# Two small first units of h in the input projection, and S5's constants made in steps beside later units

## The chip, the cores and the metric

The kernel runs on one core of a Trainium2 chip. The metric is the device time of one execution in microseconds. Its engines are named PE (TensorE, matrix products, with PEld for its weight loads), DVE (VectorE), ACT (ScalarE), POOL (GpSimd) and SP (SyncE, which here only issues transfers).

## The reference

One decoder layer on x of 256 tokens by 4096 features, all in float32:

```
shift, scale, gate = split(silu(c) @ W_ada + b_ada)       # W_ada 4096 x 12288
h = x * (1 + scale) + shift
q, k, v, g_lr, z_gla, u_s5, z_s5 = split(h @ W_in)        # W_in 4096 x 10256
o_gla = RMSNorm_head(GLA(q, k, v, alpha(g_lr))) * silu(z_gla)
o_s5  = GLU(gelu(Re(C s) + D u_s5)) * silu(z_s5)          # s: complex diagonal scan
x = LayerNorm(alpha_dn * x + gate * (concat(o_gla, o_s5) @ W_out))
```

The scan of S5 runs over groups with 64 complex states each. Its constants come from lambda and log_dt of each group: exp(lambda * dt), its powers up to the fourth, and the factor (exp(lambda * dt) - 1) / lambda.

## The kernel before

**Input projection.** h has 4096 features, 32 tiles of 128 rows (k tiles). They are made in eight *units* of four k tiles. W_in's columns are cut into 21 *chunks* of 512 columns (list KINDS; the chunk with the first head's v is cut in two, of 256 and 272 columns). A *visit* of a chunk (`win_chunk`) multiplies the k tiles of one unit, or of two units, with the chunk's weights, sums in PSUM, and at its end copies (first visit, ScalarE, L220) or adds (later visits, VectorE, L222) the sum into an accumulator in SBUF. The weights of two k tiles and one chunk are a *piece* of 512 KB: one transfer (L83, queue SP, six buffers), one cast to its high part on ScalarE (L114), one subtraction for its low part on VectorE (L115), and 12 products (L211), since float32 is made of high x high, low x high and high x low.

The plan (`win_plan`) walks through the units. In unit b some chunks are visited for unit b - 1 and unit b together, others for unit b alone. PAIRED says how many chunks share a visit at each border of two units: 6, 7, 7, 7, 7, 8, 7. So 119 visits in all.

**h.** For each unit `ada_steps` fetches x on GpSimd's queue (L161) and 32 pieces of W_ada, 512 KB each (`ada_sums`, 128 rows by 512 shift and 512 scale columns). VectorE multiplies each piece with a column of silu(c) and adds it to `rows` (L151 for the first, L153 for the others). TensorE sums `rows` over its partitions with a column of ones (L166), VectorE adds the bias (L169, L170), ScalarE makes the four tiles of h (L175) and their high parts (L176), VectorE the low parts (L177). Unit 0 is made ahead of all visits. The steps of the next unit (33: one for each piece and one for the rest) are put between the visits of the unit before, evenly by interpolation over `marks`, with a lead of ADA_LEAD = 1, which is two weight pieces ahead here. `rows` has one buffer.

**S5's constants.** `s5_params` fetches lambda and log_dt (tile lam), computes on VectorE in scratch tiles of 64 to 128 columns (tile s5scratch, lines 255 to 380), and clears pad and w0 on GpSimd (L385). It is emitted whole behind unit 0's h. `later(LATE)` lowers its priority by 60 places, and a scheduler puts its instructions between those of the projection.

**Order.** Each engine's order of instructions is fixed when the kernel is built: a list scheduler takes them by priority, which is the order of emission but for `later`, beside a simulated timeline.

Behind the projection's S5 chunks and beside its last unit come the inputs and the scan of S5, the GLA heads, the pieces of W_ada for gate, and then the products with W_out and the GLU.

Of the kernel before, what the change touches and what calls it, by code (L numbers as in the profile page):

```python
# [11 lines left out]
F32R = mybir.dt.float32r  # L12
# [6 lines left out]
P = 128  # L19
# [16 lines left out]

ADA_LEAD = 1
# [4 lines left out]
PAIRED = (6, 7, 7, 7, 7, 8, 7)  # L42
# [15 lines left out]
class Emit:  # L58
# [84 lines left out]
    def ada_sums(self, piece):  # L143

        nc = self.nc
        self.rows = rows = self.tmp([P, 1024], "rows")
        for kt in range(32):
            t = self.raw([P, 1024], self.io["ada"][piece, kt])
            c = self.silu_c[:, kt : kt + 1]
            if kt == 0:  # L150
                nc.vector.tensor_scalar(out=rows, in0=t, scalar1=c, scalar2=None, op0=ALU.mult)  # L151
            else:
                nc.vector.scalar_tensor_tensor(out=rows, in0=t, scalar=c, in1=rows, op0=ALU.mult, op1=ALU.add)  # L153
            yield

    def ada_steps(self, unit):

        nc, io = self.nc, self.io
        xs = [self.tmp([P, 2, SEQ], "x") for _ in range(2)]
        for i in range(2):  # L160
            nc.gpsimd.dma_start(out=xs[i], in_=io["xT"][:, unit * 4 + 2 * i : unit * 4 + 2 * i + 2, :])  # L161
        yield from self.ada_sums(unit)
        ps = self.xbank([P, 2, 4, 64])[:, :, :, 0]
        for s in range(2):
            for kt in range(4):
                nc.tensor.matmul(ps[:, s, kt : kt + 1], lhsT=self.rows[:, 512 * s + kt * P : 512 * s + kt * P + P],  # L166
                                 rhs=self.ones[:, 0:1], start=True, stop=True)
        m1 = self.tmp([P, 2, 4], "m1")
        nc.vector.tensor_tensor(out=m1, in0=ps, in1=self.bada[:, :, unit * 4 : unit * 4 + 4], op=ALU.add)  # L169
        nc.vector.tensor_scalar(out=m1[:, 1], in0=m1[:, 1], scalar1=1.0, scalar2=None, op0=ALU.add)  # L170
        hi = self.slot([P, 4, SEQ], F32R, "hhi")
        lo = self.slot([P, 4, SEQ], F32R, "hlo")
        for kt in range(4):
            x = xs[kt // 2][:, kt % 2]
            nc.scalar.activation(out=x, in_=x, func=AF.Identity, scale=m1[:, 1, kt : kt + 1], bias=m1[:, 0, kt : kt + 1])  # L175
            nc.scalar.copy(out=hi[:, kt], in_=x)  # L176
            nc.vector.tensor_tensor(out=lo[:, kt], in0=x, in1=hi[:, kt].bitcast(F32), op=ALU.subtract)  # L177
        self.h[unit] = (hi, lo)
        yield
# [12 lines left out]
    def win_chunk(self, idx, units, first, last):  # L192

        nc, io = self.nc, self.io
        kind, i = KINDS[idx]
        w = WIDTHS.get(kind, 512)
        ps = self.banks()
        for n, unit in enumerate(units):
            hhi, hlo = self.h[unit]
            for half in range(2):  # L200
                src = io[f"w_{kind}"][2 * unit + half] if kind in WIDTHS else io["w_in"][idx - 2 * (idx > FIRST_V), 2 * unit + half]
                whi, wlo = self.split(self.raw([P, 2, w], src))

                todo = [(m, kt, t, r) for ts in (((hhi, whi), (hlo, whi)), ((hhi, wlo),)) for m in range(2) for kt in range(2) for t, r in ts]
                begun, left = set(), [t[0] for t in todo]
                for m, kt, t, r in todo:
                    left.remove(m)
                    st = n + half == 0 and m not in begun
                    en = n == len(units) - 1 and half == 1 and m not in left
                    begun.add(m)  # L210
                    nc.tensor.matmul(ps[:, m, 0:w], lhsT=t[:, 2 * half + kt, m * P : m * P + P], rhs=r[:, kt], start=st, stop=en)  # L211
        if kind == "va":
            parts = [(self.acc["v"][0][:, :, 0:256], ps[:, :, 0:256])]
        elif kind == "vb":
            parts = [(self.acc["v"][0][:, :, 256:512], ps[:, :, 0:256]), (self.glr, ps[:, :, 256:272])]
        else:
            parts = [(self.acc[kind][i], ps)]
        for d, p in parts:
            if first:
                nc.scalar.copy(out=d, in_=p)  # L220
            else:
                nc.vector.tensor_tensor(out=d, in0=p, in1=d, op=ALU.add)  # L222
# [27 lines left out]
    def exp_exact(self, out, x, t):  # L250
# [8 lines left out]
        v.scalar_tensor_tensor(out=r, in0=n, scalar=2.12194440e-4, in1=r, op0=ALU.mult, op1=ALU.add)  # L259
        v.tensor_scalar(out=p, in0=r, scalar1=1.0 / 5040, scalar2=None, op0=ALU.mult)  # L260
        for k in (720, 120, 24, 6, 2, 1):
            v.scalar_tensor_tensor(out=p, in0=p, scalar=1.0 / k, in1=r, op0=ALU.add, op1=ALU.mult)
        v.tensor_scalar(out=p, in0=p, scalar1=1.0, scalar2=None, op0=ALU.add)
        for _ in range(2):
# [5 lines left out]
        v.tensor_copy(out=out, in_=p)  # L270

    def sincos(self, sin, cos, z, t):
# [8 lines left out]
        v.tensor_tensor(out=r2, in0=r, in1=r, op=ALU.mult)  # L281

# [4 lines left out]
        v.tensor_tensor(out=s, in0=s, in1=r, op=ALU.add)  # L287

# [4 lines left out]
        v.tensor_scalar(out=c, in0=c, scalar1=1.0, scalar2=None, op0=ALU.add)  # L293

# [5 lines left out]
        v.tensor_scalar(out=b, in0=a, scalar1=-1.0, scalar2=1.0, op0=ALU.mult, op1=ALU.add)  # L300

# [6 lines left out]
        v.tensor_tensor(out=sin, in0=r, in1=k, op=ALU.mult)  # L308

# [6 lines left out]
        v.tensor_tensor(out=cos, in0=r, in1=k, op=ALU.mult)  # L316

# [8 lines left out]
    def s5_params(self):  # L326
# [10 lines left out]
        self.exp_exact(dt, ld, (s[4], s[5], s[6], s[7], ib))  # L337
        v.tensor_tensor(out=zr, in0=lr, in1=dt, op=ALU.mult)
        v.tensor_tensor(out=zi, in0=li, in1=dt, op=ALU.mult)
        self.exp_exact(mag, zr, (s[4], s[5], s[6], s[7], ib))  # L340
# [6 lines left out]
        self.sincos(sn, cs, zi, s[4:12])  # L347
# [9 lines left out]
        v.tensor_scalar(out=nr, in0=a[:, 0], scalar1=-1.0, scalar2=None, op0=ALU.add)  # L357
        f = af[:, 0:2, 0]
# [9 lines left out]
        for k in range(1, 4):  # L368
            self.cmul(af[:, 0:2, k], a, af[:, 0:2, k - 1], t2)
        v.tensor_copy(out=pw[:, 1:3, 3], in_=a)  # L370
        for k in range(2, -1, -1):
            self.cmul(pw[:, 1:3, k], a, pw[:, 1:3, k + 1], t2)
        for o, i in ((pw[:, 0], pw[:, 2]), (af[:, 1], af[:, 1]), (af[:, 2], af[:, 0])):
            v.tensor_scalar(out=o, in0=i, scalar1=-1.0, scalar2=None, op0=ALU.mult)
        p4 = pw[:, 1:3, 0]
# [284 lines left out]
    def gate_steps(self):  # L660
# [3 lines left out]
        for qd in range(4):  # L664
            yield from self.ada_sums(8 + qd)
# [132 lines left out]
def win_plan():  # L798

    nch = len(KINDS)  # L800
    paired = [[]]
    for b in range(1, 8):
        n = PAIRED[b - 1]
        paired.append(list(range(nch - n, nch) if b % 2 == 1 else range(n)))
    paired.append([])
    plan = []
    for b in range(8):
        pairs = [(n, [b - 1, b]) for n in paired[b]]
        alone = [(n, [b]) for n in range(nch) if n not in paired[b] + paired[b + 1]]
        plan.append(alone + pairs if b == 7 else pairs + alone)  # L810
# [4 lines left out]
def hymba_layer(ctx: ExitStack, tc: tile.TileContext, io):  # L815
# [15 lines left out]
    ada = chain(*[em.ada_steps(u) for u in range(1, 8)])  # L831
    plan = win_plan()
    marks, at = [], 0
    for b, visits in enumerate(plan):
        marks.append(at)
        at += sum(len(us) for _, us in visits)
    marks[0], pos, done = 0, 0, 0
    gt = Stages((em.gate_steps(), 1))
    for b, visits in enumerate(plan):
        for n, us in visits:  # L840
            last = us[-1] == 7
# [7 lines left out]
            if b == 7:  # L849
# [32 lines left out]
def _layout(inputs):  # L882
# [10 lines left out]
    ss = w[:, : 2 * D].reshape(32, P, 2, 8, 512).transpose(3, 0, 1, 2, 4).reshape(8, 32, P, 1024)  # L893
# [54 lines left out]
```

## Time and profile before

| | us |
|---|---|
| median of 3 runs | 1745.39 |
| lowest, highest | 1734.83, 1754.34 |
| profiled execution, its own time | 1740.33 |
| its span in the trace | 1738.6 |
| mean granted TensorE clock | 0.96 |

A row of stages gives the busy time of each engine in a stretch of the span, with the number of instructions that started in it; then TensorE's granted clock as a part of full speed, the busy share of the 16 DMA engines, and GB/s. A row of a group gives line, engine, operation, what is written and read, shapes and count; then busy time in all and the mean of one in ns; then the engine's idle time just ahead of these instructions and what ended it. A row of the timeline gives start and duration, and in brackets the idle time ahead of it and its end.

### The profile page before, as it was taken

The page shows a single profiled execution, that of the slowest core. Times are in us where ns is not written, and L with a number is a line of the kernel's source. Part 1 is how long each engine was busy: PE and PEld are TensorE (multiplying, and loading weights), DVE is VectorE, ACT ScalarE, POOL GpSimd, SP SyncE. Part 2 cuts the span into 40 slices and gives each one's busy share as a digit, 9 for nine tenths or more (in the row PEclk, how much of TensorE's full clock was granted, in tenths as well). Part 3 has the DMA queues.
Part 4 walks back from the last instruction along what each step waited for, and adds up shares of the span by engine and source line. Part 5 has one row for each costly group of instructions (what it writes and reads, how often), then busy time and mean ns, then how long its engine had stood idle before and what let it go on. Part 6 is the DMA issues. An engine that isn't in the chain of part 4 may idle for free. (4 is left out here: it accounts for less than half of the span.)

```text
span 1738.6 us, 22571 instructions
## 1 busy us (share of the span) xinstructions
PE 1588.5 (91%) x7916; PEld 1316.0 (76%) x7916; DVE 1419.2 (82%) x1812; ACT 815.5 (47%) x1322; POOL 66.7 (4%) x129
## 2 busy tenths in 40 slices
PE   0689999999999999999979899889999979999995
PEld 0577878888888888887758687667786869988873
DVE  7899889898988999988869798698873537789986
ACT  0345434344343433433497556543438885433330
POOL 1000000000000000000000100000000000010000
PEclk9999999999999999999999999789997979999997
DMA  9999989999999999998967487147760336999982
GB/s 361 344 355 364 350 321 349 334 352 342 338 349 336 327 354 341 328 338 317 331 231 268 151 297 249 32 147 235 229 211 27 117 107 203 313 341 351 335 283 101
DMA packets 138386, 480.66 MB, mean 276 GB/s; under 512 B 17963, under 2 KB 18427, under 8 KB 138267
## 3 DMA queue, kind: packets, MB, share of 16 engines
q1 hardware_dynamic: 130336, 457.85, 74.1%
q0 software_dynamic: 7936, 21.37, 3.9%
q8 instruction: 62, 1.02, 0.2%
q14 instruction: 52, 0.43, 0.1%
HBM read 472.77 MB, written 6.39 MB: 276 GB/s over the span
## 5 line engine op out<-in xcount | busy, mean ns | idle before, releaser
L114 ACT CAST hi<-raw 128x1024 fp32r<-128x1024 f32 (+2 forms) x496 | 506.8, 1025 | 683.4 <-DMA raw<-in_w_in 228.0
L115 DVE TENSOR_TENSOR lo<-raw,hi 128x1024 fp32r<-128x1024 f32 (+2 forms) x496 | 583.5, 1185 | 86.5 <-ACT hi L114 80.3
L211 PE MATMUL mm<-hi,hhi 128*128 128x512 f32 (+2 forms) x1344 | 515.3, 386 | 38.0 <-ACT hi L114 32.1
L153 DVE SCALAR_TENSOR_TENSOR rows<-raw,silu_c,rows 128x1024 f32<-128x1024 f32 x372 | 476.1, 1280 | 72.1 <-DMA raw<-in_ada 69.0
L211 PE MATMUL mm<-hi,hlo 128*128 128x512 f32 (+2 forms) x1344 | 511.4, 383 | 0.0
L211 PE MATMUL mm<-lo,hhi 128*128 128x512 f32 (+2 forms) x1344 | 352.1, 384 | 0.3 <-DVE lo L115 0.2
L211 PEld LDWEIGHTS mm<-hi,hhi 128*128 128x128 f32 x1344 | 256.3, 191 | 91.5 <-ACT hi L114 35.7
L211 PEld LDWEIGHTS mm<-hi,hlo 128*128 128x128 f32 x1344 | 256.0, 190 | 48.1 <-issue 0.5
L211 PEld LDWEIGHTS mm<-lo,hhi 128*128 128x128 f32 x1344 | 247.4, 190 | 47.8 <-DVE lo L115 0.9
L689 PE MATMUL mm<-hi,ohi 128*128 128x512 f32 x512 | 203.0, 397 | 2.1 <-ACT hi L114 1.9
L689 PE MATMUL mm<-hi,olo 128*128 128x512 f32 x512 | 201.7, 394 | 0.0
L689 PE MATMUL mm<-lo,ohi 128*128 128x512 f32 x512 | 139.1, 392 | 0.0
L689 PEld LDWEIGHTS mm<-hi,ohi 128*128 128x128 f32 x512 | 97.0, 190 | 25.5 <-ACT hi L114 3.0
L689 PEld LDWEIGHTS mm<-hi,olo 128*128 128x128 f32 x512 | 96.7, 189 | 20.6 <-issue 0.7
L689 PEld LDWEIGHTS mm<-lo,ohi 128*128 128x128 f32 x512 | 95.7, 188 | 21.9 <-DVE lo L115 1.1
L545 PE MATMUL mm<-yhl,hi 128*128 128x256 f32 x512 | 68.7, 288 | 8.2 <-ACT yhl L527 7.5
L545 PEld LDWEIGHTS mm<-yhl,hi 128*128 128x128 f32 x512 | 65.3, 196 | 8.7 <-ACT yhl L527 7.7
L166 PE MATMUL px<-ones,rows 128*128 128x1 f32 x128 | 16.5, 258 | 53.7 <-DVE rows L153 53.7
L516 ACT ACTIVATE y<-pz 32x128 f32<-32x128 f32 x128 | 49.8, 389 | 25.2 <-PE pz L503 23.7
L485 ACT COPY w<-px 32x128 f32<-32x128 f32 (+3 forms) x256 | 55.5, 217 | 8.1 <-PE px L482 2.4
L166 PEld LDWEIGHTS px<-ones,rows 128*128 128x128 f32 x128 | 17.2, 209 | 54.3 <-DVE rows L153 53.7
L222 DVE TENSOR_TENSOR zsu<-mm,zsu 128x1024 f32<-128x1024 f32 x34 | 41.4, 1219 | 15.5 <-PE mm L211 15.5
(234 smaller groups left out, 1235.5 us busy)
## 6 DMA issues: line engine op xcount, KB each, us to landing
raw<-in_ada SPq DMA_DIRECT2D x384, 512.0 KB, 5.5
raw<-in_w_in SPq DMA_DIRECT2D x304, 512.0 KB, 5.4
raw<-in_w_out SPq DMA_DIRECT2D x128, 512.0 KB, 4.8
raw<-in_w_glu SPq DMA_DIRECT2D x32, 512.0 KB, 4.6
raw<-in_w_vb SPq DMA_DIRECT2D x16, 272.0 KB, 3.6
x<-in_xT POOLq DMA_DIRECT2D x16, 256.0 KB, 4.5
raw<-in_w_va SPq DMA_DIRECT2D x16, 256.0 KB, 4.1
xo<-in_x_tok POOLq DMA_DIRECT2D x8, 512.0 KB, 7.2
```

Of the source, the lines that this page charges most:

```text
L114: nc.scalar.copy(out=hi, in_=src)
L115: nc.vector.tensor_tensor(out=lo, in0=src, in1=hi.bitcast(F32), op=ALU.subtract)
L153: nc.vector.scalar_tensor_tensor(out=rows, in0=t, scalar=c, in1=rows, op0=ALU.mult, op1=ALU.add)
L166: nc.tensor.matmul(ps[:, s, kt : kt + 1], lhsT=self.rows[:, 512 * s + kt * P : 512 * s + kt * P + P], rhs=self.ones[:, 0:1], start=True, s ...
L211: nc.tensor.matmul(ps[:, m, 0:w], lhsT=t[:, 2 * half + kt, m * P : m * P + P], rhs=r[:, kt], start=st, stop=en)
L222: nc.vector.tensor_tensor(out=d, in0=p, in1=d, op=ALU.add)
L485: nc.scalar.copy(out=w0[32 * j : 32 * j + 32, n, 32 * j : P], in_=kps[32 * n : 32 * n + 32, 0 : P - 32 * j])
L516: nc.scalar.activation(out=yv[32 * a : 32 * a + 32, :, j, :], in_=yps[32 * j : 32 * j + 32, a::4, :], func=AF.Gelu_apprx_tanh)
L545: nc.tensor.matmul(ps[:, m], lhsT=w[:, kt, m * P : m * P + P], rhs=t[:, kt, :], start=u == 0 and j == 0, stop=u == 3 and j == len(todo) - 1)
L689: nc.tensor.matmul(ps[:, it], lhsT=t[:, 2 * n2 + m, it * P : it * P + P], rhs=w[:, m], start=first and j in (0, 2), stop=last and j >= len ...
```

## The change

The 32 k tiles are cut into nine units, UNITS = (2, 2, 4, 4, 4, 4, 4, 4, 4). A unit of two k tiles gets its shift and scale from 16 transfers of W_ada (`ada_short`), each 512 KB as before, with the 2 x 256 columns of two row tiles side by side; two VectorE instructions of 512 columns use one transfer. Its high and low parts share one buffer. The products of h, the weight pieces and their number stay the same; visits are 131. Eight chunks (PAIRED's first entry) are visited for units 0 and 1 together. The steps of h are placed by weight pieces in place of visits' units, with the same lead of two pieces.

`s5_params` is a generator of 21 steps of a few VectorE instructions each. One step is driven after each visit from the fourth unit on (b > 2), at the same lowered priority.

```
+UNITS = (2, 2, 4, 4, 4, 4, 4, 4, 4)
+KT0 = [sum(UNITS[:u]) for u in range(len(UNITS))]
-PAIRED = (6, 7, 7, 7, 7, 8, 7)
+PAIRED = (8, 7, 7, 7, 7, 7, 8, 7)
...
+    def ada_short(self, piece):
+        self.rows = rows = self.tmp([P, 512], "rows")
+        for k2 in range(16):
+            t = self.raw([P, 2, 512], self.io["ada_short"][piece, k2])
+            for j in range(2):
+                self.ada_row(rows, t[:, j], 2 * k2 + j)
+            yield
...
-        yield from self.ada_sums(unit)
+        yield from self.ada_short(unit) if n == 2 else self.ada_sums(unit - 2)
...
-        for kt in range(4):
+        if n == 2:
+            both = self.slot([P, 2, 2, SEQ], F32R, "hhl")
+            hi, lo = both[:, 0], both[:, 1]
+        else:
+            hi = self.slot([P, 4, SEQ], F32R, "hhi")
+            lo = self.slot([P, 4, SEQ], F32R, "hlo")
+        for kt in range(n):
...
-            for half in range(2):
+            for half in range(UNITS[unit] // 2):
+                k2 = KT0[unit] // 2 + half
...
     drive(em.ada_steps(0), 99)
     with em.later(LATE):
-        em.s5_params()
         em.ln_rows()
+    params = em.s5_params()
...
+    pieces = lambda us: sum(UNITS[u] for u in us) // 2
+    marks, steps_at, at = [], [0], 0
     for b, visits in enumerate(plan):
         marks.append(at)
-        at += sum(len(us) for _, us in visits)
+        at += sum(pieces(us) for _, us in visits)
+        if b:
+            steps_at.append(steps_at[-1] + (17 if UNITS[b] == 2 else 33))
...
-            pos += len(us)
-            want = round(33 * np.interp(pos + ADA_LEAD, marks, range(8)))
+            pos += pieces(us)
+            want = round(np.interp(pos + 2 * ADA_LEAD, marks, steps_at))
             drive(ada, want - done)
             done = max(done, want)
+            if b > 2:
+                with em.later(LATE):
+                    drive(params)
```

The remaining lines put a `yield` between the steps of `exp_exact`, `sincos` and `s5_params`, and lay out W_ada's columns for the small units on the host.

More of the change, by code (lines that the diff above doesn't have):

```diff
@@ L147, in ada_sums, with ada_row @@
         for kt in range(32):
[L148 to L153, printed above, removed]
+            self.ada_row(rows, self.raw([P, 1024], self.io["ada"][piece, kt]), kt)
+            yield
+    def ada_row(self, rows, t, kt):
+        c = self.silu_c[:, kt : kt + 1]
+        if kt == 0:
+            self.nc.vector.tensor_scalar(out=rows, in0=t, scalar1=c, scalar2=None, op0=ALU.mult)
+        else:
+            self.nc.vector.scalar_tensor_tensor(out=rows, in0=t, scalar=c, in1=rows, op0=ALU.mult, op1=ALU.add)
+    def ada_short(self, piece):
[4 more added lines that the diff above has]
+                self.ada_row(rows, t[:, j], 2 * k2 + j)
             yield
@@ L158, in ada_steps @@
         nc, io = self.nc, self.io
-        xs = [self.tmp([P, 2, SEQ], "x") for _ in range(2)]
-        for i in range(2):
-            nc.gpsimd.dma_start(out=xs[i], in_=io["xT"][:, unit * 4 + 2 * i : unit * 4 + 2 * i + 2, :])
-        yield from self.ada_sums(unit)
-        ps = self.xbank([P, 2, 4, 64])[:, :, :, 0]
-        for s in range(2):
-            for kt in range(4):
[L166 to L173, printed above, removed]
+        n, k0 = UNITS[unit], KT0[unit]
+        xs = [self.tmp([P, 2, SEQ], "x") for _ in range(n // 2)]
+        for i in range(n // 2):
+            nc.gpsimd.dma_start(out=xs[i], in_=io["xT"][:, k0 + 2 * i : k0 + 2 * i + 2, :])
+        yield from self.ada_short(unit) if n == 2 else self.ada_sums(unit - 2)
+        ps = self.xbank([P, 2, 4, 64])[:, :, 0:n, 0]
+        for s in range(2):
+            for kt in range(n):
+                at = (n * s + kt) * P
+                nc.tensor.matmul(ps[:, s, kt : kt + 1], lhsT=self.rows[:, at : at + P], rhs=self.ones[:, 0:1], start=True, stop=True)
+        m1 = self.tmp([P, 2, n], "m1")
+        nc.vector.tensor_tensor(out=m1, in0=ps, in1=self.bada[:, :, k0 : k0 + n], op=ALU.add)
+        nc.vector.tensor_scalar(out=m1[:, 1], in0=m1[:, 1], scalar1=1.0, scalar2=None, op0=ALU.add)
+        if n == 2:
+            both = self.slot([P, 2, 2, SEQ], F32R, "hhl")
+            hi, lo = both[:, 0], both[:, 1]
+        else:
+            hi = self.slot([P, 4, SEQ], F32R, "hhi")
+            lo = self.slot([P, 4, SEQ], F32R, "hlo")
+        for kt in range(n):
             x = xs[kt // 2][:, kt % 2]
@@ L199, in win_chunk @@
             hhi, hlo = self.h[unit]
-            for half in range(2):
-                src = io[f"w_{kind}"][2 * unit + half] if kind in WIDTHS else io["w_in"][idx - 2 * (idx > FIRST_V), 2 * unit + half]
+            for half in range(UNITS[unit] // 2):
+                k2 = KT0[unit] // 2 + half
+                src = io[f"w_{kind}"][k2] if kind in WIDTHS else io["w_in"][idx - 2 * (idx > FIRST_V), k2]
                 whi, wlo = self.split(self.raw([P, 2, w], src))
@@ L208, in win_chunk @@
                     st = n + half == 0 and m not in begun
-                    en = n == len(units) - 1 and half == 1 and m not in left
+                    en = n == len(units) - 1 and 2 * half + 2 == UNITS[unit] and m not in left
                     begun.add(m)
@@ L270, in exp_exact @@
         v.tensor_copy(out=out, in_=p)
+        yield
     def sincos(self, sin, cos, z, t):
@@ L316, in sincos @@
         v.tensor_tensor(out=cos, in0=r, in1=k, op=ALU.mult)
+        yield
     def cmul(self, out, a, b, t):
@@ L346, in s5_params @@
         sn, cs = s[0], s[1]
-        self.sincos(sn, cs, zi, s[4:12])
+        yield from self.sincos(sn, cs, zi, s[4:12])
         a = sc[:, 10:12]
@@ L368, in s5_params @@
         for k in range(1, 4):
+            yield
             self.cmul(af[:, 0:2, k], a, af[:, 0:2, k - 1], t2)
@@ L664, in gate_steps @@
         for qd in range(4):
-            yield from self.ada_sums(8 + qd)
+            yield from self.ada_sums(7 + qd)
             gate = self.dp.tile([1, 1024], F32, tag=f"gate{qd}", name=f"gate{qd}")
@@ L798, in win_plan @@
 def win_plan():
-    nch = len(KINDS)
+    nch, nu = len(KINDS), len(UNITS)
     paired = [[]]
-    for b in range(1, 8):
+    for b in range(1, nu):
         n = PAIRED[b - 1]
-        paired.append(list(range(nch - n, nch) if b % 2 == 1 else range(n)))
+        paired.append(list(range(nch - n, nch) if b % 2 == (nu - 1) % 2 else range(n)))
     paired.append([])
     plan = []
-    for b in range(8):
+    for b in range(nu):
         pairs = [(n, [b - 1, b]) for n in paired[b]]
         alone = [(n, [b]) for n in range(nch) if n not in paired[b] + paired[b + 1]]
-        plan.append(alone + pairs if b == 7 else pairs + alone)
+        plan.append(alone + pairs if b == nu - 1 else pairs + alone)
     return plan
@@ L830, in hymba_layer @@
     nch = len(KINDS)
-    ada = chain(*[em.ada_steps(u) for u in range(1, 8)])
+    nu = len(UNITS)
+    ada = chain(*[em.ada_steps(u) for u in range(1, nu)])
     plan = win_plan()
-    marks, at = [], 0
+    pieces = lambda us: sum(UNITS[u] for u in us) // 2
+    marks, steps_at, at = [], [0], 0
     for b, visits in enumerate(plan):
         marks.append(at)
-        at += sum(len(us) for _, us in visits)
-    marks[0], pos, done = 0, 0, 0
+        at += sum(pieces(us) for _, us in visits)
+        if b:
+            steps_at.append(steps_at[-1] + (17 if UNITS[b] == 2 else 33))
+    pos, done = 0, 0
     gt = Stages((em.gate_steps(), 1))
```

22 lines of the change are left out of this document (17 added, 5 removed).

## The prediction

> **What bounds the kernel now.** I read the totals first, then the span cut into stages, then the stretch around the change instruction by instruction.
>
> ```profile
> span 1738.6 us, 22571 instructions
> PE 1588.5 (91%) x7916; PEld 1316.0 (76%) x7916; DVE 1419.2 (82%) x1812; ACT 815.5 (47%) x1322; POOL 66.7 (4%) x129
> ...
> PE mm L689 18%; PE mm L545 5%; PE pz L503 2%; PE px L480 2%; ACT y L516 1%; PE pz L501 1%; ACT w L485 1%; DMA raw<-in_ada 0%; PE px L482 0%; DVE part L759 0%; PE mm L758 0%; DVE lo L115 0%; PE px L671 0%; ACT hi L114 0%; PE px L621 0%
> ```
>
> TensorE and VectorE are both heavily loaded, and the chain of work that ended last is mostly TensorE's. An average over stages hides where one of them gives way, so the next view has one row for each unit of the input projection (columns: length, PE, PEld, DVE, ACT, POOL busy with counts, clock, DMA share, GB/s). The cuts lie where GpSimd fetches the next x, which it does when a unit's h is ready.
>
> ```profile
> 155.45 1.21 POOL L161 DMA_DIRECT2D x<-in_xT  x2 [15.26 <-DVE hlo L177]
> 267.87 1.21 POOL L161 DMA_DIRECT2D x<-in_xT  x2 [111.20 <-DVE hlo L177]
> ```
> ```profile
> 62.00:153.00 91.00, 82.77 (x379) 68.58 (x380) 88.36 (x192) 45.88 (x53) 4.26 (x8) 1.00 0.98 357
> 153.00:268.00 115.00, 112.27 (x518) 93.84 (x518) 99.04 (x102) 52.57 (x61) 1.22 (x3) 0.99 0.93 337
> 268.00:376.00 108.00, 107.36 (x504) 89.99 (x503) 98.60 (x93) 44.55 (x49) 1.05 (x3) 1.00 0.96 347
> 376.00:492.00 116.00, 114.93 (x537) 96.21 (x537) 105.60 (x99) 46.74 (x51) 1.05 (x3) 1.00 0.93 341
> ```
>
> From 153 us on TensorE is busy 98 to 99% of the time: the bound there. In the first unit (62 to 153) VectorE is busy 88.4 of 91 us and TensorE loses 8. Before 62 us TensorE does no product of the projection at all:
>
> ```profile
> 10.68 0.75 DVE L151 TENSOR_SCALAR rows<-raw,silu_c 128x1024 f32<-128x1024 f32 x1 [9.81 <-DMA raw<-in_ada]
> 12.62 40.99 DVE L153 SCALAR_TENSOR_TENSOR rows<-raw,silu_c,rows 128x1024 f32<-128x1024 f32 x31 [1.19 <-DMA raw<-in_ada]
> ...
> 53.67 3.57 PE L166 MATMUL px<-ones,rows 128*128 128x1 f32 x16 [53.67 <-DVE rows L153]
> 57.28 0.17 DVE L169 TENSOR_TENSOR m<-px,bada 128x8 f32<-128x8 f32 x1 [3.66 <-PE px L166]
> ...
> 58.23 2.08 ACT L175 ACTIVATE x<-x,m 128x256 f32<-128x256 f32 x4 [55.45 <-DVE m L170]
> ...
> 62.66 0.80 PE L211 MATMUL mm<-hi,hhi 128*128 128x512 f32 x1 [5.42 <-ACT hi L114]
> ```
>
> It waits for 32 pieces of W_ada (L153), their sums over partitions (L166), and the four tiles of h. What fills VectorE in the first unit beside weights and pieces is S5's constants:
>
> ```profile
> 62.00:153.00 91.00, 21.67 (x123) 1.00 0.98 357
> ```
>
> That is the same view for the tile s5scratch alone (VectorE's busy time, then clock and DMA): 21.67 us in 123 small instructions.
>
> **The change part by part.** *The start.* Unit 0 needs 16 transfers in place of 32, each 512 KB as before, each used by two VectorE instructions 512 wide. Their price is not in the trace; the nearest rows are one operation at two widths:
>
> ```profile
> L399 DVE TENSOR_TENSOR ta<-ta,ta 128x512 f32<-128x512 f32 x16 | 10.9, 683 | 0.1
> ...
> L714 DVE TENSOR_TENSOR part<-part,lng 128x1024 f32<-128x1024 f32 x8 | 9.7, 1208 | 0.0
> ```
>
> Half the width takes 683 of 1208 ns, so a 1280 ns row (below) becomes 0.64 us if only width counts, 0.72 by this ratio; I take 0.70. [...]
>
> The old pieces came 40.99 / 31 = 1.32 us apart; the new pairs take 2 x 0.70 less some overlap, 1.36. So the sums end at 12.6 + 15 x 1.36 + 0.7 = 33.7 in place of 53.7. The partition sums halve (3.57 to 1.8), the h tiles halve (2.08 to 1.04): first product at about 40 in place of 62.66, **23 us earlier**.
>
> *The first three units.* TensorE's work in all is the same, so the earlier start counts only as far as the other engines keep up. Prices, from an undisturbed unit and two:
>
> ```profile
> 605.00:718.00 113.00, 110.12 (x504) 91.15 (x503) 1.00 0.94 345
> ```
> ```profile
> L115 DVE TENSOR_TENSOR lo<-raw,hi 128x1024 fp32r<-128x1024 f32 (+2 forms) x84 | 97.7, 1169 | 5.2 <-ACT hi L114 4.8
> L153 DVE SCALAR_TENSOR_TENSOR rows<-raw,silu_c,rows 128x1024 f32<-128x1024 f32 x62 | 79.3, 1279 | 1.1 <-DMA raw<-in_ada 0.5
> L222 DVE TENSOR_TENSOR zsu<-mm,zsu 128x1024 f32<-128x1024 f32 x9 | 11.0, 1222 | 6.8 <-PE mm L211 6.8
> L222 DVE TENSOR_TENSOR v<-mm,v 128x512 f32<-128x512 f32 (+1 forms) x8 | 7.6, 950 | 2.6 <-PE mm L211 2.6
> ```
>
> The first row counts L211 alone: 504 products are 42 weight pieces of 12, in 113 us: 2.69 us a piece on TensorE. The others are VectorE from 268 to 492: 1.17 us a weight piece, 1.28 a W_ada piece, up to 1.22 an addition into the accumulator (I take 1.14, since some are narrower, as the last row shows). These rows and the smaller ones like them sum to 215 us, against 98.6 + 105.6 = 204.2 busy, because neighbours overlap at their ends: factor 0.95.
>
> Units 0, 1 and 2 now take 13, 22 and 35 pieces (13 alone; 8 pairs of 2 and 6 alone; 7 pairs of 3 and 7 alone of 2):
>
> - Unit 0 (13 pieces, W_ada for unit 1): TensorE 13 x 2.69 = 35; VectorE (32 x 0.70 + 13 x 1.17 + 1) x 0.95 = 37 from 36 us on. Ends at about 75.
> - Unit 1 (22 pieces, 32 W_ada pieces): TensorE 59; VectorE (41 + 25.7 + 6 x 1.14 + 1.2) x 0.95 = 71; DMA 53 full pieces at 1.32 = 70. VectorE bounds: 71.
> - Unit 2 (35 pieces, 32 W_ada pieces): TensorE 94; VectorE (41 + 41 + 16 + 2) x 0.95 = 95; DMA 65 x 1.32 = 86. 95.
>
> 70 pieces done at 75 + 71 + 95 = 241. Before, 70 pieces (30 and 40) are done at 268. The same arithmetic on before gives 152 for the end of its first unit (155 in the trace) and 107.6 for the second (112.4), so stages run some 3 to 4% over it; with that the new mark is 249 and the **early gain 19 us**. The DMA price has another end: at a 0.98 share the first unit moved 357 GB/s, 1.47 us for 512 KB, which makes unit 1 78 us and the gain about 15; at the start it moved more:
>
> ```profile
> 20.00:30.00 10.00, 0.00 (x0) 0.00 (x0) 9.71 (x9) 0.00 (x0) 0.00 (x0) 1.00 1.03 410
> ```
>
> [...]
>
> *Additions.* There are 131 visits in place of 119, 12 more additions on VectorE. They lie in units 1 and 2 and are in the sums above.
>
> *S5's constants, moved.* 21 steps, one after each visit, fill the fourth unit (14 visits) and half of the fifth. Back to back these instructions start 0.13 us apart and last 0.19:
>
> ```profile
> 104.55 0.19 DVE L276 TENSOR_SCALAR s5scratch<-s5scratch 128x64 f32<-128x64 f32 x1
> 104.67 0.19 DVE L270 COPY s5scratch<-s5scratch 128x64 f32<-128x64 f32 x1
> 104.78 0.19 DVE L277 TENSOR_SCALAR s5scratch<-s5scratch 128x64 f32<-128x64 f32 x1
> ```
>
> So they need 16 us (123 x 0.13) to 22 us. The cover is VectorE's idle time there: 9.4 + 10.4 us in the two stages, 15 in one and a half, much of it waiting for TensorE ahead of an addition (the 6.8 us in the L222 row), where a small step fits. Over by 1 to 7; I take **4 us lost**. If none of the idle time serves, 18 are lost. Queued behind each step on VectorE are the next low weight half and the next W_ada piece; SP waits for both to free its buffers. The fetch of lam and the clearing of the pads move to GpSimd's queue in the fourth unit; GpSimd is busy 1.05 us in 108 there, and its x fetches come 100 us ahead of use. In the first stage a x fetch no longer waits for the constants; it wasn't late.
>
> *Sum.* 19 - 4 = 15 us. Behind the fifth unit the order is as before, and everything shifts. The profiled execution took 1740.33 us (span 1738.6), so 1725 on its scale; it lies 5 us under the median 1745.39, so 1730 on that one. I give **1727**.
>
> **Rivals.** What this measurement can tell from no change is about 1%, 17 us: the forecast sits on that bound.
>
> *All of it holds, nothing is lost* (0.17): the stages run at their bounds without the 4%, the steps hide. 27 us: 1713. For it, TensorE's idle time is small where nothing disturbs it:
>
> ```profile
> L211 PE MATMUL mm<-hi,hhi 128*128 128x512 f32 (+2 forms) x336 | 126.8, 380 | 1.7 <-ACT hi L114 1.7
> ```
>
> *The gain is eaten* (0.23): DMA at 1.47 leaves 15, and the constants, on a VectorE that is 91% busy, cost 15 or more: 1740 to 1746. For it: DMA shares of 0.93 to 0.98 everywhere. Against: in the first unit VectorE took the constants at 97% busy for 8 lost us.
>
> *Slower* (0.08): the 19 visits of one piece in units 0 and 1. The next visit but one needs the accumulator's bank, and the copy that frees it stands in ScalarE's queue behind a cast that waits for its transfer. The longest such waits were 2 us:
>
> ```profile
> 105.46 0.50 PE L211 MATMUL mm<-hi,hhi 128*128 128x512 f32 x1 [2.05 <-ACT hi L114]
> ```
>
> At 2.05 for each visit that is 39 us against 15: 1764. From 0.8 us a visit the change loses. Against: a visit of one piece asks of ScalarE one cast and one copy, 1.03 + 1.01 us in 2.69:
>
> ```profile
> L114 ACT CAST hi<-raw 128x1024 fp32r<-128x1024 f32 (+2 forms) x496 | 506.8, 1025 | 683.4 <-DMA raw<-in_w_in 228.0 <-PE mm L211 170.6 <-PE mm L689 161.1
> ...
> L220 ACT COPY zsu<-mm 128x1024 f32<-128x1024 f32 x8 | 8.1, 1012 | 8.8 <-PE mm L211 8.8
> ```
>
> *It doesn't do what it says* (0.04): the first product doesn't come earlier, as the weights aren't there; only the relief of VectorE in the first unit is left, 8 less 4: 1736.
>
> **How the numbers follow.** Forecast 0.48, 1718 to 1736. The range, 1708 to 1746, takes in the first rival and most of the second. Under 1728, faster by over 1%: half of the forecast's and most of its first rival's chance, 0.45. Within 1%: 0.47. Slower: 0.08.
>
> **What would show it.** L166 first at 34 us, the first L211 at 40; the x fetches of the h for the fourth unit at 245 to 253; s5scratch from there to about 420 at no more than 4 us of new TensorE idle time; the stages behind as long as before. The forecast fails if unit 1 takes over 85 us, if the fourth and fifth unit together grow by over 10, or if a later stage eats the shift.

## The result, and the profile after

The changed kernel takes **1766.61 us** (median of four executions, 1760.93 to 1771.31) against 1749.08 for the kernel before beside it (four, 1734.83 to 1754.34): ratio 1.0123, 95% interval 1.0075 to 1.0170. The forecast was 1727, range 1708 to 1746: the time is outside it and on the other side of no change. The profiled execution of after took 1766.2 us, right at its median; that of before (1740.33) lies 5 to 9 us under its own, so of the 26 us between the two traces some 17 are the kernel's.

The head of the page of after comes first. Against before, TensorE is busy 18 us longer at the same number of products, and VectorE 18 us longer.

```profile
span 1764.4 us, 22639 instructions
PE 1606.8 (91%) x7916; PEld 1322.9 (75%) x7916; DVE 1437.4 (81%) x1859; ACT 815.5 (46%) x1322; POOL 66.8 (4%) x129
```

The start came out as forecast. The timeline of after (SPq is the queue that issues the transfers):

```profile
29.93 5.05 SPq L85 DMA_DIRECT2D raw<-in_ada_short  x4
...
36.23 0.33 SPq L85 DMA_DIRECT2D raw<-in_w_va  x1
...
36.26 1.87 PE L181 MATMUL px<-ones,rows 128*128 128x1 f32 x8 [36.26 <-DVE rows L158]
...
39.55 0.33 SPq L85 DMA_DIRECT2D raw<-in_ada_short  x1
...
41.38 0.33 SPq L85 DMA_DIRECT2D raw<-in_w_vb  x1
...
41.69 2.93 PE L230 MATMUL mm<-hi,hhl 128*128 128x512 f32 x6 [3.56 <-ACT hi L116]
```

The first product of the projection starts at 41.69 in place of 62.66. But look at SP's queue: when h is ready, the buffers hold pieces of W_ada for the next small unit, and weights follow one by one between more of them. GpSimd's fetches of x, which mark that an h is ready, show how fast the lead goes:

```profile
85.60 0.55 POOL L175 DMA_DIRECT2D x<-in_xT  x1 [41.42 <-DVE hhl L195]
171.05 0.55 POOL L175 DMA_DIRECT2D x<-in_xT  x1 [84.91 <-DVE hlo L195]
...
273.32 0.54 POOL L175 DMA_DIRECT2D x<-in_xT  x1 [2.46 <-DVE hlo L195]
```

The last one was forecast for 245 to 253. To compare the kernels at equal work I count the products of the projection: 12 are one weight piece, 336 pieces in all, 70 of them in the first three units of after (two of before). The table has the times, cut to whole us, at which the n-th piece was done in each kernel's profiled execution, and the median of all its executions. Each ratio is to the executions of before that were run beside that kernel:

| kernel | 1 | 13 | 35 | 70 | 154 | 280 | 336 | median us | ratio to before, 95% interval |
|---|---|---|---|---|---|---|---|---|---|
| before | 68 | 100 | 166 | 262 | 487 | 830 | 1057 | 1749.08 | 1 |
| after | 46 | 86 | 165 | 267 | 499 | 839 | 1076 | 1766.61 | 1.0123, 1.0075 to 1.0170 |
| split_only | 46 | 87 | 169 | 271 | 497 | 835 | 1071 | 1760.44 | 1.0088, 1.0058 to 1.0118 |
| steps_only | 67 | 100 | 166 | 261 | 486 | 840 | 1070 | 1768.50 | 1.0124, 1.0087 to 1.0161 |
| cast_first | 46 | 86 | 160 | 263 | 495 | 833 | 1067 | 1768.04 | 1.0115, 1.0080 to 1.0150 |
| seven_raws | 46 | 89 | 163 | 262 | 492 | 828 | 1056 | 1758.42 | 1.0054, 1.0031 to 1.0077 |
| half_transfers | 46 | 83 | 156 | 264 | 495 | 835 | 1074 | 1763.68 | one execution |
| half_vector | 47 | 85 | 164 | 264 | 500 | 839 | 1078 | 1773.66 | one execution |
| constants_thin | 68 | 101 | 166 | 260 | 484 | 834 | 1065 | 1767.82 | 1.0142, 1.0101 to 1.0184 |
| head_behind_cast | 47 | 88 | 168 | 269 | 501 | 841 | 1070 | 1765.75 | 1.0122, 1.0085 to 1.0159 |
| nudged_before | 68 | 101 | 166 | 263 | 486 | 825 | 1058 | 1745.21 | 1.0004, 0.9969 to 1.0039 |
| before_seven_raws_g4 | 66 | 99 | 165 | 259 | 482 | 817 | 1041 | 1729.64 | 0.9922, 0.9893 to 0.9950 |
| split_seven_raws | 46 | 88 | 169 | 267 | 490 | 826 | 1055 | 1749.38 | 1.0006, 0.9982 to 1.0030 |

After is some 22 us ahead when its first piece is done, 14 at piece 13, level at piece 35 and 4 behind at piece 70. It loses 8 more beside the constants (70 to 154: 232 us in place of 224), gains 3 back up to piece 280, and loses some 16 from there to the end (925 in place of 909).

**Where the lead goes.** By the bytes moved, the forecast mark asked for a higher average rate than any kernel here has shown. The stages of before (first fence, up to piece 70 in the last row) and of after (second fence), with the columns of the earlier rows of stages:

```profile
2.00:62.00 60.00, 3.57 (x16) 3.49 (x16) 45.27 (x41) 4.02 (x12) 5.86 (x11) 1.00 0.97 367
...
2.00:262.00 260.00, 192.60 (x886) 160.91 (x887) 226.67 (x325) 99.15 (x117) 11.21 (x20) 0.99 0.96 352
```
```profile
42.00:86.00 44.00, 38.03 (x162) 30.39 (x162) 38.30 (x48) 24.14 (x30) 2.58 (x6) 0.96 0.98 336
86.00:165.00 79.00, 64.05 (x282) 50.19 (x281) 67.35 (x61) 31.64 (x36) 0.14 (x1) 0.98 0.95 356
165.00:267.00 102.00, 95.52 (x441) 77.72 (x440) 95.73 (x91) 39.49 (x45) 1.09 (x2) 1.00 0.95 345
2.00:267.00 265.00, 199.78 (x889) 160.41 (x890) 228.97 (x240) 98.67 (x117) 10.66 (x19) 0.99 0.95 345
```

Before moves 260 x 352 = 91.5 MB until piece 70, after 265 x 345 = 91.4 MB: the same 64 + 32 pieces of W_ada and 70 of weights. In the 62 us in which TensorE made no product of the projection the DMA engines were 97% busy: W_ada came then, and in after it comes later, when weights are wanted. The forecast mark of 249 is 247 us behind the start of these rows; it would have taken 91.5 / 0.247 = 370 GB/s on average, and no kernel of the table averages over 358 up to piece 70. That does not make the transfers the only bound. For the same mark TensorE's 198 us (without the sums for h ahead) would have had to fit into the 207 behind its first product, and VectorE's 229 into the 239 behind its first piece of W_ada (10.34 us). Unit 1 took 79 us for some 53 full pieces, 1.49 us each, with VectorE busy 67 of 79: which does not look like the engine that I had named; the experiments test it.

### The profile page after: what moved, and what is told of

The parts are those of the page before. It is cut to its first block, busy times and chain, and to the rows that moved or that the text cites. A ratio compares the mean times of both kernels' runs of the same rounds, so it can differ in the third digit from the quotient of the medians.

```text
span 1764.4 us, 22639 instructions
## 1 busy us (share of the span) xinstructions
PE 1606.8 (91%) x7916; PEld 1322.9 (75%) x7916; DVE 1437.4 (81%) x1859; ACT 815.5 (46%) x1322; POOL 66.8 (4%) x129
## 5 line engine op out<-in xcount | busy, mean ns | idle before, releaser
L158 DVE SCALAR_TENSOR_TENSOR rows<-raw,silu_c,rows 128x1024 f32<-128x1024 f32 (+1 forms) x403 | 483.3, 1199 | 77.1 <-DMA raw<-in_ada 72.1
L230 PE MATMUL mm<-hi,hhi 128*128 128x512 f32 (+2 forms) x1176 | 451.3, 387 | 23.7 <-ACT hi L116 22.2
L230 PE MATMUL mm<-hi,hlo 128*128 128x512 f32 (+2 forms) x1176 | 448.1, 384 | 3.0 <-DVE hlo L195 3.0
L230 PE MATMUL mm<-lo,hhi 128*128 128x512 f32 (+2 forms) x1176 | 305.1, 382 | 1.1 <-DVE lo L117 1.0
L230 PEld LDWEIGHTS mm<-hi,hhi 128*128 128x128 f32 x1176 | 224.2, 191 | 70.2 <-ACT hi L116 26.1
L230 PEld LDWEIGHTS mm<-hi,hlo 128*128 128x128 f32 x1176 | 224.3, 191 | 46.2 <-DVE hlo L195 4.3
L230 PEld LDWEIGHTS mm<-lo,hhi 128*128 128x128 f32 x1176 | 214.7, 189 | 43.3 <-DVE lo L117 2.4
L721 PEld LDWEIGHTS mm<-lo,ohi 128*128 128x128 f32 x512 | 95.5, 188 | 22.3 <-DVE lo L117 1.9
L230 PE MATMUL mm<-hi,hhl 128*128 128x512 f32 (+2 forms) x336 | 85.7, 400 | 22.5 <-ACT hi L116 19.5
L230 PEld LDWEIGHTS mm<-hi,hhl 128*128 128x128 f32 x336 | 63.2, 197 | 39.8 <-ACT hi L116 24.7
L535 PE MATMUL pz<-e,pad 128*128 128x63 f32 x256 | 50.9, 336 | 9.7 <-DVE e L492 9.7
```

The lines of the kernel that those rows point to most:

```text
L158: self.nc.vector.scalar_tensor_tensor(out=rows, in0=t, scalar=c, in1=rows, op0=ALU.mult, op1=ALU.add)
L535: nc.tensor.matmul(o[:, 1:64], lhsT=pad[:, n, ri].rearrange("p k g h -> p (k g h)"), rhs=self.e[:, 0:63, ri, pr], start=False, stop=ri == 1)
L721: nc.tensor.matmul(ps[:, it], lhsT=t[:, 2 * n2 + m, it * P : it * P + P], rhs=w[:, m], start=first and j in (0, 2), stop=last and j >= len ...
```

## The experiments

**Each part alone.** split_only keeps the units of two k tiles and makes the constants whole behind unit 0; steps_only keeps eight units of four and makes the constants in steps.

```
split_only:  drive(ada_steps(0), 99); with later(LATE): + drive(s5_params(), 99)
             - drive(params) after each visit with b > 2
steps_only:  UNITS = (4,) * 8;  PAIRED = (6, 7, 7, 7, 7, 8, 7)
```

> The two small units, with S5's constants emitted whole at their old place. If the small units themselves lose, h for the fourth unit (272 us in the changed kernel) comes no earlier than 272, at 280 to 290 if VectorE's 18 us are in the way there, and the total is no better than the changed kernel's. If the steps in the fourth and fifth unit are the loss, the total is near that of before, and h for the fourth unit still comes at 272.

> Eight units of four k tiles as before; only S5's constants are made in steps from the fourth unit on. If the early stage of the changed kernel loses because of its small units alone, this kernel keeps the relief of VectorE: the first unit ends (fetch of the next x) at about 146 us in place of 155, fourth and fifth unit together are 4 us longer, the total is about 5 us under the kernel before. If the steps are what costs, the fourth and fifth unit grow by over 10 us and the total is 10 us or more over before.

Each part loses alone, by 13 and 21 us, and together they lose 17: they don't add up. steps_only takes 22 us of VectorE work out of the first unit and gains next to nothing there (piece 35 at 166, piece 70 at 261 in place of 262), and loses in the fifth unit (below). The first row below is the first unit of before, the second that of steps_only:

```profile
62.00:152.00 90.00, 81.77 (x375) 67.73 (x376) 87.43 (x188) 44.88 (x51) 4.26 (x8) 1.00 0.98 357
```
```profile
67.00:152.00 85.00, 78.11 (x364) 64.75 (x363) 69.96 (x62) 44.89 (x52) 0.00 (x0) 0.98 0.98 361
```

VectorE falls from 97% to 82%, TensorE still idles 7 to 8 us, and the DMA share stays 0.98. VectorE alone was not what held this stage.

**Which resource holds unit 1 of after.** half_transfers fetches every second piece of W_ada for units 1 and 2 and uses it twice; half_vector fetches all but lets VectorE multiply only 16 columns of every second one; seven_raws has seven raw buffers, paid for with two of the five temporaries of 2 KB; cast_first puts a first visit's copy on ScalarE behind the first cast of the next visit.

```
half_transfers:  if kt % 2 == 0: t = self.raw(...)        # else the piece before again
half_vector:     n = 16 if kt % 2 else 1024;  ada_row(rows[:, 0:n], raw[:, 0:n], kt)
seven_raws:      RAWS 6 -> 7;  ("g2", 5) -> ("g2", 3)
cast_first:      copy(out=d, in_=p) -> held, issued with scale = a tile made from the next visit's whi
```

> The changed kernel with half of the W_ada transfers for units 1 and 2 left out (each piece that comes is used twice, so VectorE does the same instructions; shift and scale of these units are not the reference's). If the transfers and the round of the six raw buffers bound the first units (1.47 us a piece, 16 pieces fewer in unit 1), unit 1 falls from 86 us to 60 to 64, TensorE's own time, and unit 0 by 5 to 8. If VectorE's work bounds (my prediction: 71 us in unit 1), unit 1 stays at 80 us or more.

> The changed kernel with all transfers, but every second W_ada piece of units 1 and 2 is used in 16 of its columns only (shift and scale of these units are not the reference's), so VectorE has some 19 us less in unit 1 and 10 less in unit 0. If VectorE's work bounds the first units, unit 1 falls from 86 to 62 to 66 us. If the transfers bound, it stays at 80 to 86.

> The changed kernel with seven raw buffers in place of six (room from two of the five larger temporaries, which only later stages use). If the round trip of the raw buffers bounds the first units, unit 1 shrinks from 86 us towards 74 and h for the fourth unit comes at 255 to 262. If ScalarE's order or VectorE's work bounds, it comes at 268 to 274. The later stages may lose a few us for want of temporaries, so the marks of the early units decide.

> The changed kernel, but ScalarE's copy that empties PSUM after a chunk's first visit is held behind the first cast of the next visit by a data dependency (one small ScalarE instruction more per visit). If the order of copy and cast on ScalarE is what makes TensorE wait 2.05 us at the start of a visit, the first two units lose up to 20 us less: h for the fourth unit at 252 to 258 in place of 272, total 1745 to 1752. If the six raw buffers and VectorE bound there, it stays at 268 to 274 and the total stays within 6 us of the changed kernel.

The row of unit 1 (pieces 13 to 35) in half_transfers, then in half_vector, cast_first and seven_raws:

```profile
83.00:156.00 73.00, 63.35 (x273) 52.52 (x272) 67.49 (x65) 33.10 (x36) 0.55 (x1) 0.91 0.80 267
```
```profile
85.00:164.00 79.00, 66.50 (x282) 52.98 (x281) 52.13 (x62) 32.37 (x38) 0.00 (x0) 0.94 0.97 357
```
```profile
86.00:160.00 74.00, 64.01 (x280) 50.06 (x279) 66.97 (x61) 35.60 (x45) 0.00 (x0) 0.98 0.99 375
```
```profile
89.00:163.00 74.00, 63.30 (x283) 50.76 (x281) 64.03 (x60) 31.35 (x35) 0.55 (x1) 0.98 0.98 361
```

With 15 us less of VectorE work the unit takes 79 us as before. With fewer bytes, or a seventh buffer, or casts that start sooner, it takes 73 or 74. So neither VectorE nor the bare rate of the DMA engines (cast_first reached 375 GB/s with the same buffers) accounts for the last 5 or 6 us; the loop of transfer, cast, low half and free buffer fits all four runs. But half_transfers missed its 60 to 64: with the DMA share down to 0.80 the unit still takes 73, with VectorE busy 67 and TensorE 63 of them. What holds these 73 us no run separates. The copy ahead of the cast, my slower rival's mechanism, is real: after waits 13.9 us in unit 1 for such casts and the like, cast_first 9.2.

```profile
L230 PE MATMUL mm<-hi,hhl 128*128 128x512 f32 (+2 forms) x176 | 43.9, 392 | 13.9 <-ACT hi L116 11.8 <-DVE v L241 1.1 <-DVE qk L241 1.0
```
```profile
L232 PE MATMUL mm<-hi,hhl 128*128 128x512 f32 (+2 forms) x176 | 44.6, 397 | 9.2 <-ACT hi L116 7.1 <-DVE v L243 1.1 <-DVE qk L243 1.0
```

It is worth 5 us, not 39, and cast_first's total didn't move.

None of the four brought the early gain back. half_transfers lost its lead of 9 us again in unit 2 (108 us in place of 102, at a clock of 0.95); why is not settled. It has piece 70 at 264, 3 us ahead of after, with 262 x 301 = 78.9 MB moved in place of 91.4:

```profile
2.00:264.00 262.00, 200.44 (x888) 166.63 (x889) 227.24 (x239) 99.16 (x117) 10.65 (x19) 0.95 0.87 301
```

half_vector, with 25 us less of VectorE work up to piece 70, has it at 264 too, cast_first at 263 and seven_raws at 262, which is where before has it. If the transfers alone had held the first three units, 12.5 MB less would have been worth some 36 us at after's 345 GB/s. So they are one of several resources that are nearly full at the same time (unit 2 of after: TensorE 95.5 and VectorE 95.7 of 102 us, DMA share 0.95); that relieving two of them together would bring the 19 us is not shown. half_transfers and half_vector are one execution each.

**Late stages.** After has one gap in its last unit that before hasn't: the activations for the second GLA head's gate stand ahead of a weight cast on ScalarE. The casts around it:

```profile
991.10 1.04 ACT L116 CAST hi<-raw 128x1024 fp32r<-128x1024 f32 x1 [4.22 <-DMA raw<-in_w_in]
1014.85 1.03 ACT L116 CAST hi<-raw 128x1024 fp32r<-128x1024 f32 x1
```

The second cast waited for no transfer, only for its turn. nudged_before adds four one-column VectorE copies after each visit of the fifth unit to the kernel before, which gives such an order too. head_behind_cast is after with that head's first activation made to depend on the next visit's first cast.

```
nudged_before:     if b == 4: 4 x tensor_copy(out=mark, in_=h[b][1][:, 0, 0:1])
head_behind_cast:  win_chunk: after split(): gla_head(1, whi);  bias = bgate + 0 * whi[:, 0, 0:2]
```

> The kernel before, with 56 copies of one column on VectorE beside its fifth unit, some 4 us of its idle time there. By themselves they should cost nothing: under 2 us at the end of the fifth unit. They do change the order of instructions that the scheduler writes from the last units of the projection to the end of S5's outputs, about as much as the steps of S5's constants do. If that order is where the later loss of the changed kernel comes from, this kernel loses 5 to 20 us behind the fifth unit; if the later loss has to do with the steps or the small units themselves, it stays within 5 us of before.

> The changed kernel with one order on ScalarE undone: in the last unit the gate activations of the second GLA head are made to depend on the first weight cast of the next visit, so that they stand behind it in ScalarE's queue (in the changed kernel this cast stands behind them, no cast starts for 23.7 us and no product of the projection for 20.2 us, against 13.8 and 7.3 in the kernel before). If this order is the late loss: pieces 280 to 322 take 178 us in place of 188 and the total is about 1757. Rival: the gap is filled with S5's work that has to be done anyway (the kernel before with 56 small copies had a gap of 18.5 us and lost nothing in all): the gap goes and the total stays within 3 us of 1766.

nudged_before lost nothing (1.0004) with a gap of 18.5 us between products of the projection. head_behind_cast closed the gap (20.2 to 9.4 us), took 179 us in place of 188 from piece 280 to 322, and kept the total: S5's inputs, which had filled the gap, were done at 1145 as in after (1146). The gap alone is not the cause. Three more orders of the kernel before were tried, with the same four copies after each visit of another unit (b == 3, 5, 6):

> The same four copies after each visit of the fourth unit, another late order (153 rows of TensorE's order differ). If order alone makes the late loss, its size differs between the orders: 604 to 620 us from piece 280 to the end of S5's outputs, total up to 1758. If order doesn't matter: 604 to 608, total 1744 to 1748.

> The same four copies after each visit of the sixth unit, with fewer rows in another order (78 on TensorE, 39 on ScalarE; the gate activations of the second GLA head stay where they were). By order: near the kernel before, 604 to 609 us from piece 280 to the end of S5's outputs, total 1744 to 1749. By the copies' own work: 7 us more at most, and no more in this kernel than in the other two.

> The kernel before with four one-column VectorE copies after each visit of the seventh unit (56 in all, some 7 us of VectorE at most); they change the order of the instructions on TensorE and ScalarE behind them, the same gate activations of the second GLA head now stand ahead of a weight cast. If order alone makes the late loss: from piece 280 to the end of S5's outputs 612 to 620 us in place of 604, total 1750 to 1758. If order doesn't matter: 604 to 608, total 1744 to 1748.

None costs anything: 1747.82 (1.0003, 0.9969 to 1.0036), 1743.76 (0.9994, 0.9967 to 1.0021), 1744.63 (0.9981, 0.9952 to 1.0011). From piece 280 to the end the traces show, in this order, before, after, nudge_sixth, nudge_seventh and nudge_fourth:

```profile
830.00:1739.00 909.00, 835.67 (x4425) 686.31 (x4424) 681.40 (x1008) 484.81 (x951) 49.58 (x94) 0.93 0.64 217
```
```profile
839.00:1764.00 925.00, 845.97 (x4426) 693.63 (x4424) 681.70 (x1009) 484.77 (x950) 49.66 (x94) 0.91 0.63 213
```
```profile
827.00:1742.00 915.00, 843.15 (x4428) 688.59 (x4426) 681.76 (x1009) 485.44 (x953) 49.32 (x94) 0.92 0.63 216
```
```profile
825.00:1744.00 919.00, 845.40 (x4425) 691.49 (x4423) 680.51 (x1005) 483.00 (x948) 49.81 (x94) 0.92 0.63 214
```
```profile
833.00:1757.00 924.00, 850.35 (x4428) 696.76 (x4426) 681.70 (x1009) 485.72 (x953) 49.73 (x94) 0.90 0.63 214
```

The 909 of before is the lowest of all. Kernels with its work take 915 to 924 here, the longest in nudge_fourth's execution of 1758.5 us, whose median is 1747.82. nudge_seventh and nudge_fourth take 613 and 617 us from piece 280 to the end of S5's outputs, where before takes 604; so an order can lengthen that stretch in a trace, yet their medians are those of before. The lengths of the rows go roughly with TensorE's granted clock (third number from the end): 0.93 for 909, 0.92 for 915 and 919, 0.91 for after's 925, 0.90 for 924. So of the 16 us that after seems to lose late, 6 to 10 or more are before's short execution. What is left, 10 at most, isn't explained: order alone, in four other orders, was not enough, and no run separates it further.

After's loss as a whole is more than the clock of its executions. The 74 executions of before on record beside these kernels run from 1733.91 us at a mean clock of 0.962 to 1757.66 at 0.947. The six of them at 0.950 took 1746.60 to 1753.60; after's at 0.950 took 1766.2.

**The constants spread out.** constants_thin drives a step of the constants only after every third chunk (`if b > 2 and n % 3 == 0`), else as steps_only.

> The kernel before with S5's constants in the same small steps as in steps_only, but only after every third chunk, so that they reach from the fourth into the seventh unit. If a step after every visit presses VectorE too hard where it is 95% busy: pieces 112 to 196 take 229 us in place of 237, the total falls from 1768 to about 1755. Rival, the amount of VectorE work behind the first unit is what costs, wherever it lies: the loss of some 10 us moves to the sixth and seventh unit and the total stays at 1765 to 1770.

It didn't test that. Though the steps are emitted further apart, the scheduler put their VectorE instructions, whose priority is low, at nearly the same places: 38, 40, 31 and 17 scratch instructions in 373 to 430, 430 to 486, 486 to 548 and 548 to 610 us, against 38, 38, 35 and 15 in steps_only. With the same placing it lost the same (1767.82, 1768.50), so that loss doesn't hang on one build. It does not lie where most of the instructions lie. The fourth unit (pieces 112 to 154, 373 to 486 us) takes 76 of the 126 in steps_only and lasts 113 us in place of 112; the fifth (154 to 196) takes 50 and lasts 124 in place of 113. In it some 3 us are lost within three pieces of its start and 6 in its last 12 pieces, none between pieces 160 and 181. The second of these places is shown here with products of steps_only, behind the short weight pieces of 256 and 272 columns:

```profile
585.82 0.77 PE L230 MATMUL mm<-lo,hhi 128*128 128x272 f32 x4 [0.23 <-DVE lo L117]
589.54 0.79 PE L230 MATMUL mm<-hi,hhi 128*128 128x512 f32 x1 [2.95 <-ACT hi L116]
590.13 0.63 PE L230 MATMUL mm<-hi,hlo 128*128 128x512 f32 x1
590.56 0.63 PE L230 MATMUL mm<-hi,hhi 128*128 128x512 f32 x1
...
595.41 0.40 PE L230 MATMUL mm<-hi,hhi 128*128 128x512 f32 x1
595.65 0.40 PE L230 MATMUL mm<-hi,hlo 128*128 128x512 f32 x1
```

and before at the same place:

```profile
581.42 0.50 PE L211 MATMUL mm<-hi,hhi 128*128 128x512 f32 x1 [1.19 <-ACT hi L114]
581.76 0.40 PE L211 MATMUL mm<-hi,hlo 128*128 128x512 f32 x1
582.00 0.40 PE L211 MATMUL mm<-hi,hhi 128*128 128x512 f32 x1
```

VectorE is full just ahead of it (third number of the row, of steps_only):

```profile
570.00:585.00 15.00, 14.18 (x80) 11.82 (x79) 15.00 (x23) 4.65 (x6) 0.00 (x0) 1.00 0.83 274
```

The DMA share falls to 0.83 there; that late low halves keep buffers, and so hold up transfers, is argued from this, not shown. The next cast lets TensorE idle 2.95 us in place of 1.19. Behind it products start 0.43 us apart in place of 0.23, for some 5 us, so more was lost here than the idle time itself. For the 84 pieces of the two units steps_only takes 237 us (in an execution 8 us above its median), constants_thin 235 (7 below its own), before 225.

**More buffers for the kernel before.** If the loop of raw buffers binds, a seventh should help without any change to units. before_seven_raws pays with two temporaries of 2 KB (three left), before_seven_raws_g4 with one of these and one of four buffers for x and the scan's inputs, before_seven_raws_lo2 with one of three low-half buffers. split_seven_raws adds the two small units to before_seven_raws_g4, constants in place.

> The kernel before with seven raw buffers (two of five larger temporaries given up). If the round of the raw buffers bounds its first unit, that ends at 149 to 152 in place of 155.5, and the total is 3 to 6 us under before unless the later stages miss the temporaries. If the transfers themselves bound it, it still ends at 154 to 156.

> The kernel before with seven raw buffers in place of six, paid for with one of five temporaries of 2 KB and one of the four that hold x and the scan's inputs. If the missing temporaries (three in place of five) gave back the 14 us in before_seven_raws: projection done at 1043, later stages as before, total about 1733. If three buffers for x and the scan are too few, the scan stage grows by as much: 1746.

> The kernel before with seven raw buffers in place of six and two buffers for low weight halves in place of three, all temporaries kept. If low halves are seldom waited for, the projection is done at about 1045 and the total is about 1733. Rival: the seventh raw buffer only moves the wait to the low halves, as products of a low half then hold up the next one: projection not earlier, total 1750 or more.

> The two small units of the change with S5's constants whole at their old place, and with seven raw buffers paid for as in before_seven_raws_g4 (1729.6). If the raw buffers are what eats the early gain: pieces 13 to 35 take 74 us in place of 82, piece 70 is done some 6 us ahead of before_seven_raws_g4 (259), total 1724 if the late stages hold and 1735 to 1740 with the late order of split_only. If the early gain is gone for another reason: piece 70 at 262 or later, total 1740 or more.

before_seven_raws has the projection done 14 us earlier (1043) but gives it back behind (1746.19; 1.0013, 0.9983 to 1.0044). That it has too few temporaries follows from the next kernel, which pays in another way and keeps the gain. **before_seven_raws_g4 beats both kernels: 1729.64 us, 0.9922 of before, 0.9893 to 0.9950.** The products' idle time falls from 38.0 to 16.7 us (group of L211, before and then this kernel):

```profile
L211 PE MATMUL mm<-hi,hhi 128*128 128x512 f32 (+2 forms) x1344 | 515.3, 386 | 38.0 <-ACT hi L114 32.1 <-DVE qk L222 3.6 <-DVE v L222 2.4
```
```profile
L211 PE MATMUL mm<-hi,hhi 128*128 128x512 f32 (+2 forms) x1344 | 513.9, 385 | 16.7 <-ACT hi L114 14.9 <-DVE v L222 1.8
```

With two low halves the kernel takes 1814.54 (1.0412, 1.0381 to 1.0442), and the wait has moved as the rival said: 45.0 us for low halves.

```profile
L211 PE MATMUL mm<-lo,hhi 128*128 128x512 f32 (+2 forms) x1344 | 354.9, 391 | 45.4 <-DVE lo L115 45.0
```

split_seven_raws falls by its own expectation: unit 1 takes 81 us, not 74, piece 70 comes at 267, not 253, and the total (1749.38) is 0.8% over the same kernel without the split, by their ratios to before (1.0006 and 0.9922). With the constants in place VectorE is busy 77.86 of these 81 us. That fits two bounds side by side, of which taking off one isn't enough: seven_raws, with the constants moved and the seventh buffer, takes 74 there. But even its piece 70 comes only at 262.

## Why the prediction was wrong, point by point

- **Start, 23 us earlier.** Right: sums at 36.3 (34 forecast), first product at 41.69 (40). The VectorE instruction of 512 columns took 0.75 us, not 0.70, so two of them 1.50 where one of 1024 columns took 1.28.
- **Unit 0, done at 75.** It was 86. I priced VectorE and TensorE but not the transfers: 13 weight pieces and 16 of W_ada have to come, four of W_ada went ahead of the second weights in SP's queue, and the 44 us at 336 GB/s are 14.8 MB, 28 pieces, at a DMA share of 0.98.
- **Unit 1, 71 us, VectorE bounds.** It took 79, and VectorE alone did not bound it (half_vector: 79). The mis-sized term is the transfer: 1.32 us, taken from the start, where W_ada alone passes through the buffers; measured were 1.49. The other end that I named, 1.47, gave 78 and was the right one (by my own sum it left a gain of some 12, not the 15 that I wrote). half_transfers and seven_raws show that the loop of transfers and buffers is worth 5 or 6 us of it; the 73 us behind that are not explained.
- **Unit 2, 95 us.** It took 102, with TensorE busy 95.5, VectorE 95.7 and a DMA share of 0.95: I had taken the longest term alone, as if the others left it free.
- **The mark before, 268.** That is the time when the third h was ready; its 70 pieces were done just before 263. This alone makes 5 us of the 19.
- **Early gain 19.** It was a loss of 4 (split_only: 9). The step that failed is the sum 75 + 71 + 95 = 241 for the first three units: each is the longest of single terms, and the transfers were put at nothing in unit 0 and at 1.32 us a piece in unit 1. In its place the runs showed 267 us, with transfers of 1.49 us a piece in unit 1, and a DMA queue that was already 97% busy before the first product of before, while the change takes no byte out of what piece 70 needs. Transfers are not the whole of it: with 12.5 MB fewer piece 70 still came at 264, and which resources together hold these units stays open.
- **The average rate.** The first unit of before moved 357 GB/s, and I took 1.32 us a piece all the same. Shorter stretches move more (410 in 10 us at the start of before, 375 in unit 1 of cast_first), but the averages up to piece 70 lie at 340 to 358 GB/s where all of W_ada is fetched. At 357 the 91.5 MB take 91.5 / 0.357 = 256 us and the mark is 258, far nearer than mine (an estimate).
- **Constants, 4 lost.** After lost 8 in its fourth and fifth unit, steps_only 12. Inside a unit the cover that I counted served: after's fourth unit has 79 of the 126 instructions and lost 1. It did not serve where two units meet, and in the place that was looked at the idle time there was followed by products at half speed. (The three rows that I showed start 0.12 and 0.11 us apart, not 0.13.) The relief in the first unit, which I gave 8 in a rival, was 0 to 2.
- **Later stages unchanged.** They lost up to 10 us that I had not allowed for, part of it at a lower granted clock; the cause is open.
- **Rivals.** The gain eaten by transfers at 1.47 named the nearest mechanism for the early part; its time, 1740 to 1746, still had 15 us of gain in it. The slower rival's mechanism exists at an eighth of its size.

## What to carry to other kernels

When a change lets an engine start earlier, count the bytes that must have arrived by a mark common to both kernels, and divide by the rate that the mixed stage has shown; if the queue was full during the idle time (a DMA share of 0.97 here), the idle time was not free. Then hold the busy times of the other engines against the same mark: where several are each nearly full, the longest alone is too short a forecast (95 us for unit 2 here, and it took 102). Price each resource in the stage in which it will work, not where it was alone (1.32 us a piece at the start, 1.49 in unit 1). Before work is moved away from a busy engine, take it out in one run and see whether the stage gets shorter at all (half_vector: 15 us less VectorE work in unit 1, and 79 us as before).

## What the runs showed of the hardware that was not expected

- In steps_only 2.95 us of idle time on TensorE were followed by about 5 us at half speed (products 0.43 us apart, then 0.23); 1.19 us at the same place in before were not.
- One more raw buffer of 4 KB per partition, paid for with one temporary and one buffer for x and the scan, took 0.8% off the kernel (before_seven_raws_g4); the same buffer paid for with one of three low-half buffers made it 4.1% longer (before_seven_raws_lo2).
- Executions of one kernel spread over 22 us (nudge_fourth, 1736.04 to 1758.50); the trace of its highest has a TensorE clock of 0.90 from piece 280 on, against 0.92 in the other two nudges. A pair of traces can't settle 10 us.
